# A two-layer hybrid block in split fp32: joined sums, up scale on ScalarE, copies of the transposes, and a second group of seven products in one down block

## The chip, the cores and the metric

One core of a Trainium2 chip runs the whole program. The metric is the device time of one execution in microseconds (us), the median over several runs. TensorE does the matrix products, VectorE and ScalarE prepare their operands and take up their results, SyncE and GpSimd issue the transfers from the chip's memory.

## The reference

Two residual layers over 256 rows of width 2048, float32, batch 1. Each layer is a mixer followed by a gated feed-forward network (FFN) of inner width 5632. The change lies in the FFN alone:

```python
def swiglu(hn, w_gate, w_up, w_down):
    return (jax.nn.silu(hn @ w_gate) * (hn @ w_up)) @ w_down

for layer in range(DEPTH):                       # DEPTH = 2
    h = h + (gdn_rglru_mixer if layer % 2 == 0 else fox_moba_mixer)(...)
    h = h + swiglu(rmsnorm(h, ffn_norm[layer]), ffn_w_gate[layer], ffn_w_up[layer], ffn_w_down[layer])
return rmsnorm(h, final_norm)
```

`w_gate` and `w_up` are 2048 x 5632, `w_down` is 5632 x 2048.

## The kernel before

Every float32 matrix is split into a high part (`hi`, rounded) and a low part (`lo`, the rest), and a product is three matrix products: hi with hi, hi with lo, lo with hi. A weight unit is a 128 x 1024 piece: SyncE loads it (`load`, L173), ScalarE rounds it to `whi` (L179), VectorE subtracts to get `wlo` (L180), and TensorE streams it 512 columns at a time (`Bank.add`, L409 to L411) against the transposed activations, `X` or `hid`, which are held split in the same way. One unit feeds 12 matmuls of 512 columns.

The FFN goes through 11 gate/up blocks of 512 inner columns, in three stages of 4, 4 and 3, and after each stage two down blocks (p = 0 and 1) add that stage's part to the result `h`. In this text a stage's blocks are called j0, j1, j2, j3, p0, p1. A `block` (L418) has four accumulators `F00`, `F01`, `F10`, `F11` in PSUM (128 x 512 each; the first figure is the half of the rows, the second gate or up, or the half of the down columns).

Some groups of four k-tiles are not multiplied directly (8 units, 48 matmuls) but by a Winograd form of Strassen's method (`seven`, 7 products, 42 matmuls). This needs sums of weight units on VectorE (`total`, tile `T`, L384), each split again (`halves`: `thi` on ScalarE, L376; `tlo` on VectorE, L377), one sum that a GpSimd transfer adds on the way in (L443), combinations of the activations (`combine`: tiles `cf`, `cc` and `comb`, L392 to L397), four more PSUM banks `M0` to `M3`, and at the end sums of these (`ends`, tiles `e`, L462 and L464) that are added to the `F` results. In before every gate/up block except the first uses two groups of sevens; p0 uses one, p1 two in the stages of 4 and one in the stage of 3.

After a gate/up block, SiLU of the gate goes over ScalarE (L530), the up part is added and scaled on VectorE (L533, L534), and the product is transposed back in the next block: `turn` (L508, run as a hook at the next block's third unit) has 8 transposes on TensorE into two PSUM tiles `Ph` (L503), ScalarE rounds them into `hid` (L507), and VectorE subtracts (L508). I call this place the hook. `combine` of a stage's `hid` runs from hooks as well (`late`).

A scheduler puts the instructions of each engine into one fixed order; engines wait for one another by semaphores. Buffers bound how far VectorE and ScalarE run ahead: 4 for `whi`, 3 for `wlo`, 2 each for `thi`, `tlo` and `T`, 7 for raw units.

Of the kernel before, what the change touches and what calls it, by code (L numbers as in the profile page):

```python
# [11 lines left out]
T = 256  # L12
# [35 lines left out]
def body(tc, A, out):  # L48
# [338 lines left out]
    def combine(x4):  # L387

        f = mx.tile([128, 4, T], F32, name="cf", tag="T", bufs=2)
        c = mx.tile([128, 4, 2, 128], F32, name="cc4", tag="T", bufs=2)  # L390
        r = fp.tile([128, 2, 4, 2, 128], F32R, name="comb", tag="comb", bufs=4)
        V.tensor_tensor(out=f, in0=x4[:, :, 0].bitcast(F32), in1=x4[:, :, 1].bitcast(F32), op=ALU.add)  # L392
        a11, a21, a12, a22 = (f[:, 2 * j:2 * j + 2, t * 128:(t + 1) * 128] for j in range(2) for t in range(2))
        for i, (x, y) in enumerate(((a21, a22), (a21, a11), (a22, c[:, 1]), (a12, c[:, 2]))):
            V.tensor_tensor(out=c[:, i], in0=x, in1=y, op=ALU.subtract)
        S.copy(r[:, 0], c)
        V.tensor_tensor(out=r[:, 1], in0=c, in1=r[:, 0].bitcast(F32), op=ALU.subtract)  # L397
        return r

# [14 lines left out]
    def sums():  # L414

        return [[mx.tile([128, 512], F32, name=f"e{t}{i}", tag=f"e{t}{i}", bufs=1) for i in range(2)] for t in range(2)]

    def block(src, x, comb, nd, hooks, tail=0, lead=2, trail=None):  # L418
# [74 lines left out]
    def ffn(L, then, fin=None):  # L493

        gu, dn = A[f"gu{L}"], A[f"dn{L}"]
        todo, cx, ch = [], {}, {}
# [12 lines left out]

        b = 0  # L510

        for groups in ((0, 2, 2, 2), (2, 2, 2, 2), (2, 2, 2)):
            piece = len(groups)
            hid = ogp.tile([128, 16, 2, T], F32R, name="hid", tag="hid")
            late = {4: lambda hid=hid: ch.update({0: combine(hid[:, 0:4])})}
            for j in range(piece):
                hooks = {2: turn} if todo else {}
                if b == 0:
                    hooks[5] = lambda: cx.update({0: combine(X[:, 0:4])})
                    hooks[8] = rstd  # L520
                    hooks[10] = lambda: cx.update({1: combine(X[:, 4:8])})
# [4 lines left out]
                a = e or sums()  # L526
                for t in range(2):
                    if e:
                        V.tensor_tensor(out=a[t][0], in0=F[t][0], in1=e[t][0], op=(ALU.add, ALU.subtract)[t])
                    S.activation(a[t][0], a[t][0] if e else F[t][0], AF.Silu, scale=nrm["rs"][:, t:t + 1])  # L530
                for t in range(2):
                    if e:
                        V.tensor_tensor(out=a[t][1], in0=F[t][1], in1=e[t][1], op=ALU.add)  # L533
                    V.scalar_tensor_tensor(out=a[t][0], in0=a[t][1] if e else F[t][1], scalar=nrm["rs"][:, t:t + 1],  # L534
                                           in1=a[t][0], op0=ALU.mult, op1=ALU.mult)
                    todo.append((hid, j, t, a[t][0]))
                b += 1
            u0 = 2 * (b - piece)
            for p in range(2):
                end = b == NB and p == 1  # L540
                hooks = {2: turn} if todo else {}
                if p == 0 and piece == 4:
                    hooks.update(late)

                    hooks[9] = lambda hid=hid: ch.update({1: combine(hid[:, 4:8])})
                if end and fin:
                    hooks.update({5: lambda: then(0), 6: lambda: then(1)})
                last = (3, 1, 3) if end and fin else (0, 5 if 4 in hooks else 2)
# [749 lines left out]
```

## Time and profile before

| | |
|---|---|
| median of 3 runs | 2227.28 us (2226.58 to 2227.33) |
| the profiled execution's own time | 2228.4 us |
| its span in the trace | 2226.6 us |
| TensorE busy (matmul) | 2211.8 us, 99% |
| VectorE busy | 1917.1 us, 86% |
| ScalarE busy | 1284.9 us, 58% |
| granted TensorE clock | 0.999 of full speed |

A matmul's busy time overlaps its successor's, so 99% is not by itself a full engine: the distance from one start to the next shows what a matmul costs and where TensorE waited. The two FFNs take about 445 to 1110 us and 1540 to 2218 us; the mixers lie ahead of each.

### The profile page before, as it was taken

Reading aid. Unit: us, or ns where it says so; the run is one execution under the profiler, and the core shown is the slowest. Engines: PE = TensorE matmul, PEld = TensorE weight load, DVE = VectorE, ACT = ScalarE, POOL = GpSimd, SP = SyncE. Lnnn points to the kernel's source line nnn. Section 1 sums busy time; section 2 is a strip of 40 time slices with the busy share of each in tenths; the row PEclk is TensorE's granted clock in tenths of the full one; section 3 lists DMA queues with packets and bytes.
Section 4 is the critical chain, followed back from the end, with each engine's and each line's share of the span. In section 5 each row is a group of like instructions: output and inputs, shape, how many; then the busy total and the mean of one; then the engine's idle time right before and its main releaser. Section 6 shows DMA issues by size and latency. Waiting matters only on the chain.

```text
span 2226.6 us, 30372 instructions
## 1 busy us (share of the span) xinstructions
PE 2211.8 (99%) x11002; PEld 1847.0 (83%) x11002; DVE 1917.1 (86%) x2713; ACT 1284.9 (58%) x1687; POOL 50.6 (2%) x62
## 2 busy tenths in 40 slices
PE   9999999999999999999999999999999999999998
PEld 8888888888888888888878888888888888888886
DVE  8899676679999999999966658866999999999998
ACT  6776664555555665555654444545665566555565
POOL 0000000000000000000000000000000000000000
PEclk9999999999999999999999999999999999999999
DMA  7445445677777776777665455556777777777774
GB/s 281 155 146 163 141 152 184 208 223 227 212 227 231 220 233 211 225 230 225 193 196 171 161 169 175 168 178 185 223 226 216 221 225 238 219 214 239 218 236 151
DMA packets 125992, 451.67 MB, mean 203 GB/s; under 512 B 14065, under 2 KB 15601, under 8 KB 125713
## 3 DMA queue, kind: packets, MB, share of 16 engines
q1 hardware_dynamic: 117488, 420.10, 58.3%
q0 software_dynamic: 8064, 29.36, 7.8%
q8 instruction: 86, 1.41, 0.3%
q14 instruction: 66, 0.53, 0.1%
q10 hardware_dynamic: 288, 0.27, 0.0%
HBM read 447.58 MB, written 2.10 MB: 202 GB/s over the span
## 4 chain that ended last, share of the span: by engine, by line
PE 95%; DVE 2%; issue 1%; ACT 1%; DMA 1%; DVEq 0%; ACTq 0%
PE F L411 15%; PE F L410 15%; PE F L409 15%; PE Pw L199 10%; PE Pw L204 5%; PE Px L303 5%; PE Px L304 5%; PE Px L305 5%; PE M L410 5%; PE M L411 4%; PE M L409 4%; PE Ph L503 1%; DVE wlo L180 1%; PE Psc L1068 1%; PE Pt L326 0%
## 5 line engine op out<-in xcount | busy, mean ns | idle before, releaser
L179 ACT CAST whi<-raw 128x1024 fp32r<-128x1024 f32 x720 | 755.3, 1051 | 666.8 <-PE F L411 263.8
L180 DVE TENSOR_TENSOR wlo<-raw,whi 128x1024 fp32r<-128x1024 f32 x720 | 874.5, 1219 | 189.3 <-PE Px L304 70.1
L199 PE MATMUL Pw<-X,whi 128*128 128x512 f32 x1088 | 388.3, 400 | 0.0
L409 PE MATMUL F<-whi,X 128*128 128x512 f32 x848 | 331.4, 391 | 0.0
L410 PE MATMUL F<-wlo,X 128*128 128x512 f32 x848 | 330.4, 390 | 0.0
L411 PE MATMUL F<-whi,X 128*128 128x512 f32 x848 | 330.0, 389 | 0.0
L204 PE MATMUL Pw<-X,wlo 128*128 128x256 f32 x1088 | 304.8, 280 | 1.0 <-DVE wlo L180 0.9
L376 ACT CAST thi<-T 128x1024 fp32r<-128x1024 f32 x168 | 176.6, 1051 | 124.1 <-DVE T L384 84.0
L199 PEld LDWEIGHTS Pw<-X,whi 128*128 128x128 f32 x1088 | 204.2, 188 | 47.7 <-issue 0.5
L377 DVE TENSOR_TENSOR tlo<-T,thi 128x1024 fp32r<-128x1024 f32 x168 | 205.1, 1221 | 28.0 <-ACT thi L376 27.3
L204 PEld LDWEIGHTS Pw<-X,wlo 128*128 128x128 f32 x1088 | 205.3, 189 | 2.4 <-DVE wlo L180 2.0
L409 PE MATMUL F<-whi,hid 128*128 128x512 f32 x480 | 187.5, 391 | 0.0
L411 PE MATMUL F<-whi,hid 128*128 128x512 f32 x480 | 186.9, 389 | 0.0
L410 PE MATMUL F<-wlo,hid 128*128 128x512 f32 x480 | 186.8, 389 | 0.0
L411 PEld LDWEIGHTS F<-whi,X 128*128 128x128 f32 x848 | 159.2, 188 | 33.1
L409 PEld LDWEIGHTS F<-whi,X 128*128 128x128 f32 x848 | 159.2, 188 | 32.7
L410 PEld LDWEIGHTS F<-wlo,X 128*128 128x128 f32 x848 | 159.2, 188 | 32.4
L384 DVE TENSOR_TENSOR T<-T,raw 128x1024 f32<-128x1024 f32 x112 | 136.5, 1219 | 1.1 <-DMA raw<-in_gu 0.2
L410 PE MATMUL M<-tlo,comb 128*128 128x512 f32 x336 | 131.8, 392 | 1.1 <-DVE tlo L377 1.0
L409 PE MATMUL M<-thi,comb 128*128 128x512 f32 x336 | 131.4, 391 | 0.0
L411 PE MATMUL M<-thi,comb 128*128 128x512 f32 x336 | 130.9, 390 | 0.0
L411 PEld LDWEIGHTS F<-whi,hid 128*128 128x128 f32 x480 | 90.1, 188 | 18.8
(389 smaller groups left out, 3409.5 us busy)
## 6 DMA issues: line engine op xcount, KB each, us to landing
raw<-in_gu SPq DMA_DIRECT2D x352, 512.0 KB, 4.4
raw<-in_dn SPq DMA_DIRECT2D x176, 512.0 KB, 4.4
raw<-in_w0w SPq DMA_DIRECT2D x72, 512.0 KB, 3.6
raw<-in_wo SPq DMA_DIRECT2D x64, 512.0 KB, 3.6
raw<-in_w1w SPq DMA_DIRECT2D x64, 512.0 KB, 3.6
raw<-in_gu POOLq DMA_DIRECT2D x40, 512.0 KB, 6.8
raw<-in_w1x SPq DMA_DIRECT2D x32, 512.0 KB, 3.7
raw<-in_w0x SPq DMA_DIRECT2D x16, 512.0 KB, 3.6
```

What stands on the lines that cost most here:

```text
L179: S.copy(hi, raw)
L180: V.tensor_sub(lo, raw, hi.bitcast(F32))
L199: PE.matmul(P.rearrange("p a b -> p (a b)"), hi[:, kk], X[:, k].rearrange("p a b -> p (a b)"), start=k == 0, stop=False)
L204: PE.matmul(P[:, 0], lo[:, kk], X[:, k, 0], start=False, stop=k == NK - 1)
L303: PE.matmul(Ps[t], x[:, 0, ts], hi[:, kk], start=k == 0, stop=False)
L304: PE.matmul(Ps[t], x[:, 0, ts], lo[:, kk], start=False, stop=False)
L376: S.copy(hi, t)
L377: V.tensor_sub(lo, t, hi.bitcast(F32))
L384: V.tensor_tensor(out=t, in0=a, in1=b, op=ALU.add)
L409: PE.matmul(self.t, xh, hi[:, kk], start=self.i == kk == 0, stop=False)
L410: PE.matmul(self.t, xh, lo[:, kk], start=False, stop=False)
L411: PE.matmul(self.t, xl, hi[:, kk], start=False, stop=kk == 1 and self.i == self.n - 1)
```

## The change

Four edits, all in `combine`, `sums`, `ends` and `ffn`.

1. The four `e` tiles become one tile `e` of 128 x 4 x 512. In `ends`, two of the four narrow sums are joined into one of 2 x 512 that reads `M1` twice; after down blocks the four additions of `h` become two of 1024.
2. The up part's scale moves from VectorE (L534) to a ScalarE activation, and the product of gate and up becomes one multiplication of 2 x 512.
3. The combinations of `hid` no longer add the split halves again (`cf<-hid`, L392): in `turn`, ScalarE makes two more copies of the transposes straight into a tile `cf`. The combinations move from the down block p0 and its hooks into the gate/up blocks j1 and j2 (j1 alone in the stage of 3), hook 6.
4. In the first stage of each FFN, p0 uses two groups of sevens instead of one.

```diff
+    def whole():
+        return mx.tile([128, 4, T], F32, name="cf", tag="T", bufs=2)
-    def combine(x4):
-        f = mx.tile([128, 4, T], F32, name="cf", tag="T", bufs=2)
+    def combine(f):
...
-        V.tensor_tensor(out=f, in0=x4[:, :, 0].bitcast(F32), in1=x4[:, :, 1].bitcast(F32), op=ALU.add)
...
     def sums():
-        return [[mx.tile([128, 512], F32, name=f"e{t}{i}", tag=f"e{t}{i}", bufs=1) for i in range(2)] for t in range(2)]
+        return mx.tile([128, 4, 512], F32, name="e", tag="e", bufs=1)
...
         def ends():
-            (c1, w5), (v, w7) = sums()
-            S.copy(c1, M[0].t)
-            for o, a, b, op in ((v, M[2], c1, ALU.subtract), (w5, M[1], v, ALU.add), (v, M[3], v, ALU.add), (w7, M[3], w5, ALU.add)):
-                V.tensor_tensor(out=o, in0=a.t, in1=b, op=op)
+            e = sums()
+            S.copy(e[:, 0], M[0].t)
+            V.tensor_tensor(out=e[:, 1], in0=M[2].t, in1=e[:, 0], op=ALU.add)
+            V.tensor_tensor(out=e[:, 2], in0=M[3].t, in1=e[:, 1], op=ALU.add)
+            V.tensor_tensor(out=e[:, 1::2], in0=M[1].t.rearrange("p (a n) -> p a n", a=1).to_broadcast([128, 2, 512]),
+                            in1=e[:, 1:3], op=ALU.subtract)
...
         def turn():
...
+            if j < wanted[0]:
+                cf[j] = whole()
+                for t, (P, d) in enumerate(Ps):
+                    S.copy(cf[j][:, :, t * 128:(t + 1) * 128], P)
...
-                if j == 1 and piece == 3:
-                    hooks[6] = late[4]
+                if 0 < j <= wanted[0]:
+                    hooks[6] = chs(j - 1)
...
+                for i, f in enumerate((AF.Silu, AF.Copy)):
+                    for t in range(2):
+                        if e is not None:
+                            V.tensor_tensor(out=a[:, 2 * t + i], in0=F[t][i], in1=a[:, 2 * t + i], op=ALU.add)
+                        S.activation(a[:, 2 * t + i], F[t][i] if e is None else a[:, 2 * t + i], f, scale=nrm["rs"][:, t:t + 1])
+                V.tensor_tensor(out=a[:, 0::2], in0=a[:, 1::2], in1=a[:, 0::2], op=ALU.mult)
...
-                if p == 0 and piece == 4:
-                    hooks.update(late)
-                    hooks[9] = lambda hid=hid: ch.update({1: combine(hid[:, 4:8])})
...
-                             {m: lambda m=m: ch[m] for m in range(1 + (p == 1 and piece == 4))}, piece, hooks, *last)
+                             {m: lambda m=m: ch[m] for m in range(2 if both or p == 1 and piece == 4 else 1)}, piece, hooks, *last)
...
+                    V.tensor_tensor(out=et, in0=h[:, t, c], in1=et, op=ALU.add)
```

The first place is ScalarE's order at the hook of j2 in the first FFN's first stage, with what each row waits for. Before:

```order
L179 CAST whi<-raw_5498 128x1024 [waits DMAHW4_49,DVE_49,PE_49]
L507 CAST hid<-Ph 128x4x128 [waits PE_49] x2
L376 CAST thi<-T 128x1024 [waits DVE_49]
L179 CAST whi<-raw_5525 128x1024 [waits DMAHW7_49,PE_49,Activation_49]
L376 CAST thi<-raw_5377 128x1024 [waits DMASW2_49,PE_49]
```

And of the change:

```order
L179 CAST whi<-raw_5507 128x1024 [waits DMAHW4_49,PE_49,Activation_49]
L517 CAST hid<-Ph 128x4x128 [waits PE_49] x2
L523 COPY cf<-Ph 128x4x128 [waits DVE_49] x2
L179 CAST whi<-raw_5534 128x1024 [waits DMAHW6_49,PE_49,Activation_49]
L376 CAST thi<-T 128x1024 [waits DVE_49]
L376 CAST thi<-raw_5383 128x1024 [waits DMASW2_49,PE_49,Activation_49]
```

Two copies stand between the casts of the transposes and the next `thi`, and each of the two waits for VectorE.

The second place is VectorE's order at the same hook. Before:

```order
L384 TENSOR_TENSOR T<-T,raw_5447 128x1024
L180 TENSOR_TENSOR wlo<-raw,whi 128x1024
L384 TENSOR_TENSOR T<-raw_5498,raw 128x1024
L508 TENSOR_TENSOR hid<-Ph,hid 128x4x128 x2
L377 TENSOR_TENSOR tlo<-T,thi 128x1024
L180 TENSOR_TENSOR wlo<-raw_5498,whi 128x1024
L377 TENSOR_TENSOR tlo<-raw_5377,thi 128x1024
```

And of the change:

```order
L180 TENSOR_TENSOR wlo<-raw_5456,whi 128x1024
L377 TENSOR_TENSOR tlo<-T,thi 128x1024
L180 TENSOR_TENSOR wlo<-raw,whi 128x1024
L518 TENSOR_TENSOR hid<-Ph,hid 128x4x128 x2
L384 TENSOR_TENSOR T<-T,raw_5456 128x1024
L180 TENSOR_TENSOR wlo<-raw_5507,whi 128x1024
L377 TENSOR_TENSOR tlo<-T,thi 128x1024
L377 TENSOR_TENSOR tlo<-raw_5383,thi 128x1024
```

The last sum of the first group and the first sum of the second stood ahead of the `hid` rows and now stand behind them; after the hook the two `tlo` that TensorE asks for next are the third and fourth wide rows, where they were the first and third.

## Rows read from the trace of the kernel before

**Rows 1.** The page: the span, and busy time of each engine.
```profile
span 2226.6 us, 30372 instructions
PE 2211.8 (99%) x11002; PEld 1847.0 (83%) x11002; DVE 1917.1 (86%) x2713; ACT 1284.9 (58%) x1687; POOL 50.6 (2%) x62
```

**Rows 2.** Timeline of TensorE: start, duration, line, operation, count, idle before and releaser.
```profile
578.20 0.39 PE L410 MATMUL F<-wlo,X 128*128 128x512 f32 x1
...
579.01 0.39 PE L411 MATMUL M<-thi,comb 128*128 128x512 f32 x1
...
704.30 0.39 PE L409 MATMUL F<-whi,X 128*128 128x512 f32 x1
...
717.90 0.39 PE L409 MATMUL M<-thi,comb 128*128 128x512 f32 x1
...
718.63 0.40 PE L411 MATMUL M<-thi,comb 128*128 128x512 f32 x1
...
968.62 0.39 PE L409 MATMUL F<-whi,X 128*128 128x512 f32 x1
...
970.10 0.40 PE L411 MATMUL M<-thi,comb 128*128 128x512 f32 x1
...
1810.04 0.40 PE L409 MATMUL M<-thi,comb 128*128 128x512 f32 x1
...
1811.00 0.40 PE L411 MATMUL M<-thi,comb 128*128 128x512 f32 x1
```

**Rows 3.** Waits of TensorE's weight loads, whole span: us in total, times, longest.
```profile
PEld M L410 <- DVE tlo L377: 4.0, 8, 1.2
...
PEld F L410 <- DVE tlo L377: 1.2, 6, 0.2
PEld M L409 <- DVE hid L508: 1.0, 4, 0.4
PEld M L409 <- ACT thi L376: 1.0, 4, 0.3
```

**Rows 4.** Windows of j1, j2, j3, p0, p1 of stage one: length, engines' busy, counts.
```profile
478.00:519.70 41.70, 41.70 (x190) 34.58 (x189) 37.33 (x38) 25.27 (x28) 1.73 (x2) 1.00 0.76 225
519.70:561.40 41.70, 41.70 (x190) 34.56 (x189) 39.06 (x40) 24.20 (x27) 1.73 (x2) 1.00 0.75 227
561.40:603.00 41.60, 41.52 (x187) 33.92 (x186) 40.53 (x45) 24.59 (x28) 0.86 (x1) 1.00 0.68 215
603.00:646.00 43.00, 43.00 (x196) 35.69 (x195) 40.87 (x47) 23.07 (x25) 1.72 (x2) 1.00 0.72 211
646.00:687.00 41.00, 41.00 (x183) 33.89 (x182) 38.27 (x40) 22.25 (x23) 0.86 (x1) 1.00 0.78 231
```

**Rows 5.** Timeline of VectorE behind the hook of j3, and two later rows.
```profile
572.80 1.28 DVE L508 TENSOR_TENSOR hid<-Ph,hid 128x512 fp32r<-128x512 f32 x2
574.00 1.21 DVE L377 TENSOR_TENSOR tlo<-T,thi 128x1024 fp32r<-128x1024 f32 x1
575.13 1.22 DVE L180 TENSOR_TENSOR wlo<-raw,whi 128x1024 fp32r<-128x1024 f32 x1
576.27 1.22 DVE L392 TENSOR_TENSOR cf<-hid 128x1024 f32<-128x1024 f32 x1
577.40 1.22 DVE L377 TENSOR_TENSOR tlo<-raw,thi 128x1024 fp32r<-128x1024 f32 x1
...
626.12 0.75 DVE L395 TENSOR_TENSOR cc<-cf 128x256 f32<-128x256 f32 x2
```

**Rows 6.** Waits of VectorE in the first FFN, 446 to 1100 us.
```profile
DVE tlo L377 <- ACT thi L376: 17.7, 30, 1.4
```

**Rows 7.** Timeline of all engines at the hook of j2.
```profile
528.19 1.03 PE L503 MATMUL Ph<-tab,e 128*128 128x128 f32 x8
...
529.34 1.07 ACT L507 CAST hid<-Ph 128x512 fp32r<-128x512 f32 x2
...
530.49 1.28 DVE L508 TENSOR_TENSOR hid<-Ph,hid 128x512 fp32r<-128x512 f32 x2
```

More of the change, by code (lines that the diff above doesn't have):

```diff
@@ L398, in combine, with combine_x @@
         return r
+    def combine_x(x4):
+        f = whole()
+        V.tensor_tensor(out=f, in0=x4[:, :, 0].bitcast(F32), in1=x4[:, :, 1].bitcast(F32), op=ALU.add)
+        return combine(f)
     class Bank:
@@ L495, in ffn @@
         gu, dn = A[f"gu{L}"], A[f"dn{L}"]
-        todo, cx, ch = [], {}, {}
+        todo, cx, ch, cf = [], {}, {}, {}
         def turn():
@@ L514, in ffn @@
             hid = ogp.tile([128, 16, 2, T], F32R, name="hid", tag="hid")
-            late = {4: lambda hid=hid: ch.update({0: combine(hid[:, 0:4])})}
+            both, wanted[0] = b == 0, piece - 2
+            chs = lambda m: lambda: ch.update({m: combine(cf.pop(m))})
             for j in range(piece):
@@ L518, in ffn @@
                 if b == 0:
-                    hooks[5] = lambda: cx.update({0: combine(X[:, 0:4])})
+                    hooks[5] = lambda: cx.update({0: combine_x(X[:, 0:4])})
                     hooks[8] = rstd
-                    hooks[10] = lambda: cx.update({1: combine(X[:, 4:8])})
-                if j == 1 and piece == 3:
-                    hooks[6] = late[4]
+                    hooks[10] = lambda: cx.update({1: combine_x(X[:, 4:8])})
+                if 0 < j <= wanted[0]:
+                    hooks[6] = chs(j - 1)
                 F, e = block(lambda i, u: gu[b, u, i], lambda k: X[:, k], {m: lambda m=m: cx[m] for m in range(groups[j])}, 4, hooks)
-                a = e or sums()
-                for t in range(2):
[L528 to L536, printed above, removed]
+                a = sums() if e is None else e
+                for i, f in enumerate((AF.Silu, AF.Copy)):
[4 more added lines that the diff above has]
+                V.tensor_tensor(out=a[:, 0::2], in0=a[:, 1::2], in1=a[:, 0::2], op=ALU.mult)
+                for t in range(2):
+                    todo.append((hid, j, t, a[:, 2 * t]))
                 b += 1
@@ L541, in ffn @@
                 hooks = {2: turn} if todo else {}
-                if p == 0 and piece == 4:
-                    hooks.update(late)
-                    hooks[9] = lambda hid=hid: ch.update({1: combine(hid[:, 4:8])})
                 if end and fin:
                     hooks.update({5: lambda: then(0), 6: lambda: then(1)})
-                last = (3, 1, 3) if end and fin else (0, 5 if 4 in hooks else 2)
+                last = (3, 1, 3) if end and fin else ()
                 F, e = block(lambda i, u: dn[2 * p + i, u0 + u], lambda k: hid[:, k],
-                             {m: lambda m=m: ch[m] for m in range(1 + (p == 1 and piece == 4))}, piece, hooks, *last)
+                             {m: lambda m=m: ch[m] for m in range(2 if both or p == 1 and piece == 4 else 1)}, piece, hooks, *last)
+                c = slice(2 * p * 512, (2 * p + 2) * 512)
+                for t in range(2):
+                    et = e[:, 2 * t:2 * t + 2].rearrange("p a n -> p (a n)")
+                    V.tensor_tensor(out=et, in0=h[:, t, c], in1=et, op=ALU.add)
                 hs = [[h[:, t, (2 * p + i) * 512:(2 * p + i + 1) * 512] for i in range(2)] for t in range(2)]
-                for t in range(2):
-                    for i in range(2):
-                        V.tensor_tensor(out=e[t][i], in0=hs[t][i], in1=e[t][i], op=ALU.subtract if t > i else ALU.add)
                 if end and fin:
                     with tc.manual_schedule(engines={V.engine, S.engine}):
-                        fin(lambda t, i: V.tensor_tensor(out=hs[t][i], in0=F[t][i], in1=e[t][i], op=ALU.add))
+                        fin(lambda t, i: V.tensor_tensor(out=hs[t][i], in0=F[t][i], in1=e[:, 2 * t + i], op=ALU.add))
                     continue
@@ L560, in ffn @@
                     for i in range(2):
-                        V.tensor_tensor(out=hs[t][i], in0=F[t][i], in1=e[t][i], op=ALU.add)
+                        V.tensor_tensor(out=hs[t][i], in0=F[t][i], in1=e[:, 2 * t + i], op=ALU.add)
                 if b == NB and not fin:
```

8 lines of the change are left out of this document (4 added, 4 removed).

## The prediction

> **What bounds the kernel now.** I read the page first [rows 1]: TensorE is busy for 99% of the span, VectorE for 86%, ScalarE for 58%. Since matmuls overlap, the next view is the timeline of TensorE [rows 2]: from 704.30 to 717.90 us lie 60 matmuls of 512 columns, so one start follows another after 13.60/60 = 0.2267 us. That pitch is the price of a matmul as long as its operands are there, and nearly every gap in both FFNs has it. What breaks it are five places, all in the FFNs, where TensorE waits for a `tlo` of VectorE. Over two steps, 0.453 us without a wait, it took 0.81 us at 578.20, 0.73 at 717.90, 1.48 at 968.62 and 0.96 at 1810.04; the fifth, at 1670, is the second FFN's twin of 578 and as long. The loss is 0.36 + 0.28 + 1.03 + 0.36 + 0.51 = 2.5 us. The waits of the weight loads [rows 3] give the outer bound: all that they waited for `tlo`, `thi` and `hid` is 4.0 + 1.2 + 1.0 + 1.0 = 7.2 us, in 22 waits, and a weight load runs ahead of its matmul, so not all of it was lost.
>
> So TensorE's own work is the bound, with little to win from waiting; but VectorE is close behind. The windows of five blocks [rows 4] show it busy for 37.3, 39.1, 40.5, 40.9 and 38.3 us of 41.7, 41.7, 41.6, 43.0 and 41.0, and it also idles where a `tlo` must wait for the `thi` that ScalarE makes from the sum just before: 17.7 us over 654 us [rows 6], 1.1 us in a block of 41.7 us. In j3, 40.5 + 1.1 = 41.6 is the whole window: that is where the 0.36 us at 578.20 went, and behind its hook [rows 5] stand `hid` twice, `tlo`, `wlo`, the sum `cf`, and only then the late `tlo`, at 577.40.
>
> **The change part by part.** *Matmuls.* A group of sevens has 42 matmuls where plain units have 48. One more group in each FFN removes 12 matmuls: 12 x 0.2267 = 2.72 us, wholly on the path. The other edits touch no matmul.
>
> *VectorE's work.* By starts [rows 5] a row of 1024 elements costs 1.13 us, one of 512 costs 0.60 (1.20 for two), one of 256 about 0.37 (0.75 for two). The joined sums turn 4 x 0.60 = 2.40 into 2 x 0.60 + 1.13 = 2.33, in 32 blocks; the up scale turns six narrow rows (3.6) into four and a wide one (3.53), in 20 blocks; the sums with `h` turn 8 narrow rows into 4 and 2 wide ones, 0.14 less in 12 blocks. The sums `cf` go: 10 x 1.13. A new group adds 10 wide rows where 8 plain units had 8: 2 x 2.27. In all 2.2 + 1.4 + 1.7 + 11.3 - 4.5 = 12 us less. The row of 2 x 512 that reads a bank twice is not in the trace; between 0.60 (one row of 512) and 1.28 (two rows as they stand, [rows 5]) I take the wide row's 1.13. None of this is on the path; it counts only where VectorE is late.
>
> *Where it lies.* A combination without its sum is 4 x 0.37 + 1.13 = 2.6 us, and it moves. By block [rows 4]: j1 37.3 + 2.6 - 0.1 = 39.8; j2 39.1 + 2.6 - 0.1 = 41.6; j3 40.5 - 3.7 - 0.1 = 36.7 (the first `cf` and its combination stood here); p0 40.9 - 3.7 + 2.3 - 0.2 = 39.3; p1 38.1. The sum is about the same, but j2 becomes the fullest: with 1.1 us of forced idle 42.7 us in 41.7 us. The stage of 3 and the blocks behind p1 get lighter, so the waits at 717.90, 968.62 and 1810.04 should go, and so should the two in j3: 2.5 us back.
>
> *New waits.* In j2 VectorE falls 1.0 us behind. Its order is less kind there too: two sums now stand behind `hid`, and the two `tlo` that TensorE asks for next are the third and fourth wide rows. j3 of before, filled to the brim, lost 0.36 us; j2 with 1.0 us more would lose up to 1.4, or nothing if the operands made ahead absorb it. I take 0.7, the middle, since the rows give no nearer one. There are two such stages in each FFN (the stage of 3 combines one group only, and without the sum): 4 x 0.7 = 2.8 us, with bounds 0 and 5.6.
>
> *ScalarE.* Two copies at ten hooks and two more activations in each of 22 blocks; by the two casts of 1.07 us [rows 7] a pass is 0.53, so a block gains some 1.07 + 1.07 + 1.05 = 3.2 us on 25 of 41.7 us [rows 4]. That is covered by idle time. What is not covered is the order: each copy waits for VectorE's read of the same `Ph`, and behind it stand the next `whi` and `thi`. At the hook of j2 [rows 7] the casts ended at 529.34 + 1.07 = 530.41 and VectorE read from 530.49 to 531.77. The copies would end near 532.3, so ScalarE comes free 1.9 us later. I count it at nothing beyond the 0.7 us: the `thi` behind it are asked for about 6.5 us after `Ph` began (8 transposes, 1.03 us by their row, then 24 matmuls, 5.4 us), at 528.19 + 6.5 = 534.7, and two casts after 532.3 the first is ready at 534.4. It is just in time, and each delay of VectorE's read passes on one to one.
>
> Here the Trainium skill bears on the case: *PSUM — Partial Sum Buffer*, "PSUM bank collisions raise a hardware error", says that two engines must not touch one bank and quadrant at once, reads against reads included. The trace agrees as far as it goes: the reads of `Ph` by ScalarE end at 530.41 and VectorE's begin at 530.49 [rows 7], though another row of VectorE may have set that moment. Were the copies free to read beside VectorE, they would end near 531.5, 0.8 us sooner, and the term of 2.8 us would shrink to some 0 to 2; with the rule it stands.
>
> *The sum.* The profiled execution took 2228.4 us, its span 2226.6 us. 2228.4 - 2.7 - 2.5 + 2.8 = 2226.0. The median of the runs, 2227.28 us, is 1.1 us below the profiled one, so the forecast is 2224.9 us, 2.4 us or 0.11% less. The mixers keep their order, and the tail its rows; they count nothing.
>
> **The rivals.** A difference under 0.2%, 4.5 us, is about what a measurement of this kernel can't tell from none.
>
> *All waits go.* VectorE's 12 us less is enough, j2's excess is absorbed by the buffers, and no new wait shows: 2227.3 - 2.7 - 2.5 = 2222.1 us. For it: the load of the whole stage doesn't rise and 1.0 us is less than one unit's 2.7 us. Against it: the j3 of before lost time without any excess.
>
> *Nothing comes of it.* The old waits stay, because j0 behind p1 was late for a transfer rather than for work, and j2 pays 2.8 us: 2227.3 - 2.7 + 2.8 = 2227.4 us. For it: the longest of them, 1.03 us, is one of a kind, with no twin in the second FFN. Against it: the blocks ahead of it lose work.
>
> *Slower: the copies hold up ScalarE.* At ten hooks ScalarE is free 1.9 us later, and what I called just in time is late: VectorE's `tlo` wait for `thi`, its lateness moves the next read of `Ph`, and the next copies with it. If half of the 1.9 us comes out at TensorE at every hook, that is 9.5 us: 2227.3 - 2.7 - 2.5 + 2.8 + 9.5 = 2234.4 us. It decides from about 0.7 us a hook on. For it: the waits stand in the order, and VectorE in j2 has no reserve. Against it: in j1 and in the stage of 3 the next `thi` that matters is asked for later.
>
> **How the numbers follow.** Forecast 0.48, all waits go 0.22, nothing comes of it 0.22, slower 0.08. The forecast and the third case lie within 0.2%: 0.70 for the same. All waits go gives faster by more than 4.5 us: 0.22. The last gives slower: 0.08. The forecast's own range is 2222.5 (new waits 0.4 in all) to 2227.7 (5.6 of them). The range for 8 in 10 takes in the first rival and the third, and leaves the slower one out: 2221.5 to 2229.0 us. Its ends lie beyond the cases by about half a microsecond below, and above by what a quarter of the slower rival's term would add.
>
> **What would show it.** Right: 12 fewer matmuls at a pitch of 0.2267 us; no wait left at the places in j0 behind p1; waits for `tlo` in j2 or at the hook of j3, in the first two stages of each FFN, together 2 to 4 us; VectorE's busy time 12 us lower, ScalarE's higher by some 30 us. Wrong: waits for `thi` or `tlo` behind the copies at most hooks, half a microsecond and more each; or a profile in which weight loads wait no longer at all; or VectorE's row of 2 x 512 much above 1.13 us.

## The result: 0.5% slower, and the profile after

The changed kernel takes 2238.9 us (median of 6 runs, 2234.3 to 2239.6), the kernel before beside it 2226.4 us (6 runs): ratio 1.0051, 95% interval 1.0041 to 1.0061. By that ratio it is 11.4 us longer (the medians differ by 12.5); every "us over before" below is worked out from a ratio in this way. The forecast was 2.4 us less, with a range that ended at 2229.0 us. The page of the changed kernel, against [rows 1]:

```profile
span 2237.7 us, 30300 instructions
...
PE 2218.7 (99%) x10990; PEld 1841.3 (82%) x10990; DVE 1909.6 (85%) x2637; ACT 1331.7 (60%) x1757; POOL 52.4 (2%) x64
```

TensorE has 12 matmuls fewer, as foreseen, and VectorE works 7.5 us less; yet the span grew by 11.1 us. So TensorE waits some 13.8 us more. Its timeline shows where, in the manner of [rows 2]:

```profile
595.38 0.39 PE L417 MATMUL F<-whi,X 128*128 128x512 f32 x1
595.61 0.39 PE L418 MATMUL F<-wlo,X 128*128 128x512 f32 x1
596.63 0.50 PE L417 MATMUL F<-thi,X 128*128 128x512 f32 x1 [0.64 <-ACT thi L376]
...
2193.05 0.39 PE L419 MATMUL F<-whi,hid 128*128 128x512 f32 x1
2195.51 0.49 PE L417 MATMUL F<-whi,hid 128*128 128x512 f32 x1 [2.07 <-DVE h L572]
2195.81 0.61 PE L418 MATMUL F<-wlo,hid 128*128 128x512 f32 x1
2196.22 0.63 PE L419 MATMUL F<-whi,hid 128*128 128x512 f32 x1
2196.65 0.63 PE L417 MATMUL F<-whi,hid 128*128 128x512 f32 x1
```

At 595.61, in j3, the next start comes 1.02 us later instead of 0.227; at 2193.05, where p0 ends and p1 begins in the last stage, 2.46 us later, and behind it starts stand up to 0.43 apart. The waits of the weight loads have also grown, those for ScalarE's `thi` most: 11.1 us in these rows, where [rows 3] has 1.0; those for `tlo` rose from 5.2 to 8.5:

```profile
PEld M L417 <- ACT thi L376: 7.1, 23, 0.6
PEld M L418 <- DVE tlo L377: 5.1, 12, 1.0
PEld F L417 <- ACT thi L376: 4.0, 8, 1.2
PEld F L418 <- DVE tlo L377: 3.4, 14, 0.5
```

For the comparison of many kernels I add up, for each block, the time between one start of a 512-column matmul and the next, less 0.2267 us, and call it the block's loss; a step that holds the transposes of the hook is left out. Both FFNs together, in us (1j2 is j2 of the first stage). The runs are described in the next section; u stands for the changed kernel with a part undone, b for the kernel before with a part done, a for the changed kernel altered:

| kernel | ratio to before [95%] | 1j0, 1j1 | 1j2, 1j3 | 1p0, 1p1 | 2j0, 3j0 | 2j1 | 2j2, 2j3 | 2p0, 2p1 | 3j1, 3j2 | 3p0, 3p1 | all |
|---|---|---|---|---|---|---|---|---|---|---|---|
| before | 1 | 0.8 | 1.4 | 0.2 | 2.5 | 0.5 | 0.8 | 0.2 | 1.1 | 0.8 | 8.3 |
| after | 1.0051 [41, 61] | 0.9 | 4.6 | 1.8 | 2.8 | 1.7 | 3.0 | 0.2 | 2.6 | 4.8 | 22.2 |
| b1 | 1.0027 [18, 35] | 0.7 | 3.8 | 0.2 | 2.3 | 0.6 | 2.7 | 0.2 | 1.2 | 0.8 | 12.5 |
| b2 | 1.0032 [20, 45] | 0.9 | 3.1 | 0.2 | 2.7 | 3.0 | 4.5 | 0.2 | 1.8 | 0.8 | 17.2 |
| b3 | 1.0020 [11, 30] | 5.1 | 1.1 | 0.2 | 1.8 | 0.3 | 0.8 | 0.2 | 1.3 | 0.7 | 11.5 |
| b4 | 1.0075 [62, 87] | 0.7 | 1.3 | 6.6 | 2.2 | 1.0 | 2.0 | 7.0 | 1.4 | 0.9 | 23.1 |
| b5 | 1.0013 [4, 22] | 0.7 | 1.5 | 0.3 | 1.5 | 0.6 | 3.1 | 0.3 | 1.6 | 0.8 | 10.2 |
| b6 | 1.0013 [4, 21] | 0.8 | 1.4 | 0.5 | 1.4 | 0.6 | 3.0 | 0.2 | 1.1 | 0.8 | 9.7 |
| b7 | 1.0077 [63, 90] | 0.8 | 1.5 | 8.8 | 8.6 | 0.6 | 3.0 | 0.2 | 1.0 | 0.8 | 25.4 |
| b8 | 1.0024 [15, 33] | 0.7 | 1.4 | 1.4 | 0.5 | 1.6 | 1.0 | 0.6 | 1.1 | 3.4 | 11.7 |
| b9 | 1.0071 [59, 84] | 0.7 | 2.0 | 7.0 | 1.6 | 0.8 | 2.0 | 5.1 | 1.5 | 0.8 | 21.5 |
| b10 | 1.0018 [9, 26] | 0.8 | 1.2 | 0.2 | 0.7 | 1.8 | 1.3 | 0.2 | 1.1 | 2.5 | 9.7 |
| u1 | 1.0075 [63, 88] | 0.8 | 4.9 | 1.6 | 1.8 | 1.3 | 3.0 | 8.9 | 2.1 | 0.8 | 25.2 |
| u2 | 1.0027 [15, 38] | 0.8 | 3.5 | 1.4 | 2.0 | 2.1 | 2.8 | 2.7 | 2.2 | 1.5 | 19.0 |
| u3 | 1.0040 [26, 54] | 3.4 | 1.9 | 1.9 | 1.9 | 0.6 | 4.3 | 0.7 | 1.7 | 0.9 | 17.3 |
| u4 | 1.0045 [32, 57] | 0.8 | 4.6 | 2.3 | 1.5 | 1.4 | 3.2 | 0.2 | 2.2 | 1.2 | 17.5 |
| u234 | 1.0044 [32, 57] | 0.7 | 5.4 | 0.2 | 1.3 | 0.5 | 3.3 | 0.2 | 2.3 | 5.2 | 19.0 |
| a1 | 1.0026 [17, 35] | 0.9 | 1.7 | 1.5 | 1.3 | 1.6 | 1.7 | 0.8 | 2.1 | 1.0 | 12.6 |
| a2 | 1.0028 [16, 39] | 0.8 | 1.6 | 1.7 | 2.5 | 1.3 | 1.7 | 0.2 | 2.4 | 1.1 | 13.2 |
| a3 | 1.0078 [64, 92] | 0.9 | 1.6 | 6.1 | 7.6 | 2.5 | 1.2 | 0.2 | 2.5 | 3.1 | 25.7 |

(The interval's two figures are its last digits: [41, 61] is 1.0041 to 1.0061. Losses are of one profiled run each, which for the changed kernel took 2239.5 us, near the upper end of its six; the ratio is of all runs, of b3's without one execution of 6690.6 us.) For the changed kernel the row closes: 22.2 - 8.3 - 12 x 0.2267 = 11.2 us against 11.1 us of span.

### The profile page after: what moved, and what is told of

Its sections match the earlier page's. It is cut to its first block, busy times and chain, and to the rows that moved or that the text cites. A ratio compares the mean times of both kernels' runs of the same rounds, so it can differ in the third digit from the quotient of the medians.

```text
span 2237.7 us, 30300 instructions
## 1 busy us (share of the span) xinstructions
PE 2218.7 (99%) x10990; PEld 1841.3 (82%) x10990; DVE 1909.6 (85%) x2637; ACT 1331.7 (60%) x1757; POOL 52.4 (2%) x64
## 4 chain that ended last, share of the span: by engine, by line
PE 94%; DVE 3%; issue 1%; ACT 1%; DMA 1%; DVEq 0%; ACTq 0%; SPq 0%
PE F L418 15%; PE F L417 15%; PE F L419 15%; PE Pw L199 10%; PE Pw L204 5%; PE M L418 5%; PE Px L303 5%; PE M L417 5%; PE Px L305 5%; PE Px L304 5%; PE M L419 4%; PE Ph L513 1%; DVE wlo L180 1%; PE Psc L1079 1%; PE Pt L326 0%
## 5 line engine op out<-in xcount | busy, mean ns | idle before, releaser
L376 ACT CAST thi<-T 128x1024 fp32r<-128x1024 f32 x174 | 183.4, 1054 | 143.7 <-DVE T L384 115.7
L377 DVE TENSOR_TENSOR tlo<-T,thi 128x1024 fp32r<-128x1024 f32 x174 | 212.5, 1221 | 33.3 <-ACT thi L376 32.3
L417 PE MATMUL F<-whi,hid 128*128 128x512 f32 x452 | 177.2, 392 | 2.1 <-DVE h L572 2.1
L418 PE MATMUL F<-wlo,hid 128*128 128x512 f32 x452 | 176.8, 391 | 0.0
L419 PE MATMUL F<-whi,hid 128*128 128x512 f32 x452 | 176.8, 391 | 0.0
L384 DVE TENSOR_TENSOR T<-T,raw 128x1024 f32<-128x1024 f32 x116 | 141.5, 1219 | 0.9 <-DMA raw<-in_gu 0.5
L417 PE MATMUL M<-thi,comb 128*128 128x512 f32 x348 | 138.0, 397 | 0.5 <-ACT thi L376 0.4
L418 PE MATMUL M<-tlo,comb 128*128 128x512 f32 x348 | 136.9, 393 | 0.8 <-DVE tlo L377 0.8
L419 PE MATMUL M<-thi,comb 128*128 128x512 f32 x348 | 135.7, 390 | 0.0
L417 PEld LDWEIGHTS F<-whi,hid 128*128 128x128 f32 x452 | 85.3, 189 | 20.0 <-issue 2.5
```

The source lines that it names most:

```text
L376: S.copy(hi, t)
L377: V.tensor_sub(lo, t, hi.bitcast(F32))
L384: V.tensor_tensor(out=t, in0=a, in1=b, op=ALU.add)
L417: PE.matmul(self.t, xh, hi[:, kk], start=self.i == kk == 0, stop=False)
L418: PE.matmul(self.t, xh, lo[:, kk], start=False, stop=False)
L419: PE.matmul(self.t, xl, hi[:, kk], start=False, stop=kk == 1 and self.i == self.n - 1)
```

## The experiments

**Undoing one part of the changed kernel (u1 to u4).** Each run's expectation, printed before its result, sets theories against one another. Theory A blamed ScalarE's copies, B the second group, C the joined sums at the seam of p0 and p1, D the up scale; E, added for the second round, blamed the place of the combinations.

u1, the sums with `h` narrow again:

```diff
-                    V.tensor_tensor(out=et, in0=h[:, t, c], in1=et, op=ALU.add)
+                    for i in range(2):
+                        V.tensor_tensor(out=e[:, 2 * t + i], in0=hs[t][i], in1=e[:, 2 * t + i], op=ALU.add)
```

> The changed kernel with one part undone: the sums with h stand as four rows of 512 instead of two of 1024. Theory C (order of VectorE at the seam between p0 and p1: in the stage of 3 of the second FFN TensorE waited 2.46 us at 2193 us for the sum that frees F00, and the next matmuls came at half pitch): the pause there goes and the time falls by about 3.9 us, from 2238.9 to 2235.0. Theories A, B and D (the loss is made by ScalarE's copies, by the second group, or by the up scale): the pause may stay, the time stays within 1.5 us of 2238.9.

Measured: the pause at 2193 us went (3p0, 3p1: 4.8 to 0.8), but the kernel became slower still, 16.7 us over before: p1 of the second stage now loses 4.1 us in one FFN and 4.7 in the other (2p1), at two pauses some 16 us into the block and a lower clock behind them. C is right on the place and wrong on the time. At the first of these places, where the next start after 915.75 comes 1.32 us later, ScalarE's timeline shows a late weight unit, and right behind it the `thi` that TensorE waits for:

```profile
915.02 1.05 ACT L179 CAST whi<-raw 128x1024 fp32r<-128x1024 f32 x1 [4.55 <-DMA raw<-in_dn]
915.98 1.03 ACT L376 CAST thi<-raw 128x1024 fp32r<-128x1024 f32 x1
```

The windows around it (window, length, busy time of TensorE, its weight loads, VectorE, ScalarE and GpSimd, granted clock, share of the DMA engines, GB/s):

```profile
912.00:914.00 2.00, 2.00 (x11) 1.65 (x10) 1.15 (x1) 0.00 (x0) 0.00 (x0) 1.00 1.02 268
914.00:916.00 2.00, 2.00 (x10) 1.44 (x8) 0.00 (x0) 0.98 (x2) 0.00 (x0) 1.00 1.03 416
916.00:918.00 2.00, 0.64 (x2) 0.19 (x1) 0.95 (x1) 2.00 (x4) 0.00 (x0) 1.00 0.95 387
```

From 912 to 916 VectorE is busy for 1.15 us and ScalarE for 0.98, and the DMA engines run at full share: a weight unit, not an engine, is what all wait for.

u2, the up scale on VectorE again (`scalar_tensor_tensor` for each half, as in before L534):

> The changed kernel with one part undone: the up scale and the product stand on VectorE again, one narrow row for each half. Theory D (two more activations a block stand ahead of the casts on ScalarE, so thi and whi come late and the many small waits of 0.1 to 0.4 us appear): the small waits go, some 4 to 6 us less, 2233 to 2235. Theory A (the copies of Ph hold ScalarE up) and theory B (the second group of sevens in p0 of the first stage, with its transfers): no more than 1 us either way, since ScalarE has 40% of idle time and VectorE's work stays the same; 2238 to 2240.

Measured: 6.0 us over before, 5 us less than the change: as D said. That the waits of j2 and j3 stay (3.5 and 2.8) speaks against D's mechanism.

u3, no copies; `combine` sums `hid` at the same hooks:

```diff
-            if j < wanted[0]:
-                cf[j] = whole()
...
-            chs = lambda m: lambda: ch.update({m: combine(cf.pop(m))})
+            chs = lambda m, hid=hid: lambda: ch.update({m: combine_x(hid[:, 4 * m:4 * m + 4])})
```

> The changed kernel with one part undone: no copies of Ph on ScalarE; the combinations sum hid again on VectorE, at the same hooks. Theory A (each copy waits for VectorE's read of the same Ph, and the next whi and thi stand behind it): the waits at j3 of the first stage (1.4 us in each FFN) and at j0 of the second stage shrink, 4 to 8 us less, 2231 to 2235, although VectorE has 11 us more work. Theory B (second group, transfers) or C (the seam of p0 and p1): those waits stay, and with VectorE fuller in j1 and j2 the time is the same or up to 3 us longer, 2238 to 2242.

Measured: 8.9 us over before, 2.5 less, with overlapping intervals: short of the 4 to 8 us less that A said. 1j3 got better (3.7 to 0.8), 1j1 and 2j3 worse.

u4, `both = False`:

> The changed kernel with one part undone: p0 of the first stage has one group of sevens again (12 matmuls more in all, 2.7 us of TensorE); combinations and copies stay. Theory B (the second group puts 10 wide rows and 7 late transfers where 8 plain units stood, and its loss exceeds its 2.7 us): the time falls, 2234 to 2238. Theories A, C and D: only the 12 matmuls come back, 2.7 us longer, 2241 to 2242.

Measured: 10.0 us over before, though 12 matmuls came back. So the group's 2.7 us are used up by waits in the changed kernel, as B said; its interval overlaps the change's.

No single undoing brought the time back to before's. So the parts were done one by one on the kernel before.

**One part alone (b1 to b3, and u234).** b1 moves the combinations, with their sum on VectorE; b2 also makes them from copies; b3 has the up scale alone (`S.activation(..., AF.Copy, scale=rs)` and a narrow product); u234 is the changed kernel with u2, u3 and u4 together.

```diff
-                if j == 1 and piece == 3:
-                    hooks[6] = late[4]
+                if 0 < j <= piece - 2:
+                    hooks[6] = chs(j - 1)
...
-                if p == 0 and piece == 4:
-                    hooks.update(late)
-                    hooks[9] = lambda hid=hid: ch.update({1: combine(hid[:, 4:8])})
...
-                last = (3, 1, 3) if end and fin else (0, 5 if 4 in hooks else 2)
+                last = (3, 1, 3) if end and fin else ()
```

The last edit lets p0's groups begin three units earlier. The changed kernel has it too; the section on the change doesn't list it.

> The kernel before with one part done alone: the combinations of hid stand where the changed kernel has them (at the seventh unit of j1 and j2, in the stage of 3 of j1), with their sum on VectorE; no copies, no second group, no joined sums, no up scale on ScalarE. Theory A (the copies) and theory D (the up scale): nothing of the loss is here, within 1.5 us of before; VectorE is fuller in j1 and j2 and may lose 1 to 2 us there, but p0 gains what it had lost. Theory E (the loss comes from where the combinations stand): 4 to 8 us longer than before.

> The kernel before with the combinations moved and made from ScalarE's copies of Ph, nothing else. Theory A (the copies stand behind VectorE's read of the same Ph and hold whi and thi up): 4 to 6 us longer than before, waits of about 1 us behind the hook of j3 in the first stage of each FFN; more than the kernel that only moves them. Theory D (the up scale): within 1.5 us of before, since 11 us of VectorE's work are gone.

> The kernel before with the up scale alone on ScalarE, the product on VectorE; nothing else. Theory D (two more activations at every seam between two blocks hold thi and whi up): 4 to 6 us longer than before. Theory A (the copies): within 1 us of before.

> The changed kernel with three parts undone: up scale on VectorE, no copies, one group in p0 of the first stage. What is left beside the kernel before are the joined sums and the moved combinations. Theory C (joined sums change VectorE's order at the seams): 3 to 5 us longer than before and than the kernel that only moves the combinations. Theories A and D: within 1.5 us of the latter.

Measured: b1 6.0 us, b2 7.1, b3 4.5, u234 9.8 us over before. A falls as the main cause: the copies add 1.1 us to the moved combinations, less than the intervals' width. E holds: the place of the combinations alone costs more than half of the whole, in 1j2, 1j3 (+2.4) and 2j2, 2j3 (+1.9). D's price holds, but at one place only, where j1 of the first stage follows j0 (0.8 to 5.1). TensorE's timeline of b3 there:

```profile
492.70 0.39 PE L411 MATMUL F<-thi,X 128*128 128x512 f32 x1
493.64 0.49 PE L409 MATMUL M<-thi,comb 128*128 128x512 f32 x1 [0.55 <-ACT thi L376]
494.89 0.50 PE L410 MATMUL M<-tlo,comb 128*128 128x512 f32 x1 [0.76 <-DVE tlo L377]
```

The changed kernel has nothing at that place (0.9), so b3's price isn't a term of its time.

**Which move, and which sum (b4 to b7).** b4: the joined sums alone. b5: only the first combination moved, to j1. b6: the two in j1 and j3 (`if j == 1 or j == 3: hooks[6] = chs(j // 2)`). b7: b6 with the second group in p0.

> The kernel before with the joined sums alone (the row that reads a bank twice, and two rows of 1024 instead of four of 512 for the sums with h); combinations, up scale and groups as before. Theory C (F00 is freed later, since its sum with h now waits for the whole chain of sums: a pause of TensorE of 2 to 3 us at the seam of p0 and p1 in the stage of 3 of the second FFN, and half clock behind it): 3 to 5 us longer than before, with the pause at that place alone. Theory E (all of the loss stands where the combinations stand): within 1 us of before.

> The kernel before with only the first combination of hid moved, to the seventh unit of j1; the second stays in p0 and p0 keeps its late groups. Moving both cost 6 us, most of it in j2 and j3. Theory E1 (the second combination, in j2, fills VectorE there, and the loss comes out at j3): less than 2 us longer than before, and j3 as before or better. Theory E2 (the loss comes from p0's groups of sevens, which begin three units earlier): also less than 2 us. Theory E3 (any combination ahead of the hook costs the next block 1 us): 3 us longer.

> The kernel before with the first combination at the seventh unit of j1 and the second at that of j3 instead of j2, p0's groups three units earlier. Theory E1 (j2 is too full with a combination in it): VectorE's work by block is then 41, 39, 41, 37 us, j2 and j3 keep the excess of before, and the time is within 2 us of before. Theory E2 (p0's groups that begin earlier) or E3 (any block behind a combination): 4 to 6 us longer, as when both were moved to j1 and j2.

> As the kernel with the combinations in j1 and j3, and a second group of sevens in p0 of the first stage (12 matmuls less, 2.7 us). If its ten wide rows on VectorE are covered in p0 and p1: 2.7 us less than that kernel, 1 to 3 us less than before. If the second group pays as it does in the changed kernel (0.4 us in p0 and 0.4 us in p1 of each FFN): 1.2 us less than the kernel without it, about the time of before.

Measured: b5 and b6 2.9 us over before, b4 16.7, b7 17.1. E1 holds for the second half of b1's 6 us: with the second combination out of j2, 1j2 and 1j3 keep the loss of before (1.4), though the 2.9 us left are more than E1's 2. They stay with the first combination, in 2j2 and 2j3 (E3 in part). E2 falls, since b6, with p0's groups three units earlier, costs no more than b5, which left them in their place. Joined sums and second group both cost 14 us and more here, nearly all of it in p0, p1 or just behind: no theory foresaw that size. In b4, where TensorE pauses at 661.84, ScalarE waits for a weight unit as in u1 (its timeline), and the DMA engines are again at a share of 0.91 to 1.03 (658 to 664 us), though VectorE is busy here until 662 us:

```profile
661.99 1.05 ACT L179 CAST whi<-raw 128x1024 fp32r<-128x1024 f32 x1 [2.50 <-DMA raw<-in_dn]
662.94 1.04 ACT L376 CAST thi<-raw 128x1024 fp32r<-128x1024 f32 x1
```

**The joined sums taken apart, and the second combination moved within the changed kernel (b8 to b10, a1).** b8 has the one tile `e` and the signs, all rows narrow; b9 adds the row that reads `M1` twice, b10 the rows of 1024 with `h`. a1 is the changed kernel with the second combination in j3, made from a sum on VectorE instead of copies.

```diff
-            both, wanted[0] = b == 0, piece - 2
-            chs = lambda m: lambda: ch.update({m: combine(cf.pop(m))})
+            both, wanted[0] = b == 0, 1
+            chs = lambda m, hid=hid: lambda: ch.update({m: combine_x(hid[:, 4 * m:4 * m + 4]) if m else combine(cf.pop(m))})
...
-                if 0 < j <= wanted[0]:
-                    hooks[6] = chs(j - 1)
+                if j == 1 or j == 3:
+                    hooks[6] = chs(j // 2)
```

> The kernel before with the four sums kept in one tile of 4x512 instead of four tiles, and the signs that go with it; every row of VectorE has its old size. Theory C1 (the size of the joined rows makes the pauses: they stand in one piece in front of the rows that free raw buffers): within 1.5 us of before. Theory C2 (it is the one tile: the next block's sums may not begin before the last reader of all four halves is done, and that shifts VectorE's order): most of the 16.7 us of the joined sums, 2238 to 2244, with the pauses of 2 to 4 us in p1.

> The kernel before with the joined row that reads a bank twice (and the one tile), sums with h narrow as before. Theory C1a (the row of 2 x 512 is the cause): 10 us or more longer than before, pauses in p1. Theory C1b (the two rows of 1024 with h are): within 2 us of the kernel with the one tile alone.

> The kernel before with the two rows of 1024 with h (and the one tile), the sums of a block's end narrow as before. Theory C1b (F00, and the rows behind it, wait for a row that needs the whole chain of sums): 10 us or more longer than before, pauses in p1 behind late transfers. Theory C1a: within 2 us of the kernel with the one tile alone.

> The changed kernel with the second combination of hid at the seventh unit of j3 instead of j2, from a sum on VectorE (the first stays in j1, from ScalarE's copies). Theory E1 (a combination in j2 fills VectorE there, and j2 and j3 of the first two stages lose 5.3 us more than before): these waits fall to 2 us or less in all, and the time by 3 us or more, unless p0, which follows j3 and has two groups now, takes it back as in the kernel with the combinations in j1 and j3 and two groups. Theory A (the copies): also less, since half of them go, but j1 stays as it is and j2 and j3 fall by no more than half.

Measured: b8 5.3, b9 15.8, b10 4.0 us over before. The one tile alone costs more than C1 said and less than C2. On the kernel before it is the row that reads the bank twice that costs most (C1a), and yet not by its own price: it is busy for 1.22 us, as any wide row, in b9 and in the changed kernel alike (b9's groups by line: count, busy time, mean ns of one, idle time before):

```profile
L465 DVE TENSOR_TENSOR e<-M,e 128x1024 f32<-128x1024 f32 x32 | 39.2, 1224 | 0.8
```

a1 is 5.8 us over before, 5.6 less than the change: 1j2 and 1j3 fall from 4.6 to 1.7, 2j2 and 2j3 from 3.0 to 1.7, as E1 said, though it had 2 us in all and 3.4 are left. a1 also has fewer copies, so by itself it doesn't part the place from them; the place alone is what b6 has against b1, both without copies, and there it is worth 3.1 us.

**Do the repairs add up (a2, a3)?** a2 is a1 with the up scale on VectorE, a3 is a2 with narrow sums at a block's end.

> The changed kernel with two parts altered: the second combination at the seventh unit of j3, from a sum on VectorE, and the up scale on VectorE again. If the two repairs add up (5.6 us for the place of the combination, 5.3 us for the up scale): 11.4 - 10.9 = 0.5 us longer than before. If they repair the same waits: 4 to 6 us longer than before, as the first of them alone.

> As the kernel with the combination in j3 and the up scale on VectorE, and the sums at a block's end narrow again (two rows of 512 instead of the row that reads a bank twice). Theory C1a inside the changed kernel (that row costs there too, as it did alone on the kernel before): 3 us or more less than without this edit, so below the time of before. If the row matters only where the combinations stand in p0 as before: within 1.5 us of the kernel without this edit. All that is then left of the change are the second group (2.7 us less of TensorE), the first combination from copies, and the rows of 1024 with h.

Measured: a2 6.2 us over before, a3 17.4. They don't add up: u2's 5 us are worth nothing on top of a1. Both theories on a3 miss: the row that cost b9 some 10 us more than b8 now saves 11. a3, without it, is with b7 the slowest of all, by waits in p0 and p1 of the first stage and in j0 behind them (13.7 us in these columns). No kernel that was run beats the one before.

**What the second combination does.** GpSimd's timeline has the transfer that adds a weight unit on its way in (start, duration, idle before and releaser). Before:

```profile
554.78 0.86 POOL L443 DMA_DIRECT2D raw<-in_gu  x1 [22.82 <-DMA raw<-in_gu]
573.41 0.86 POOL L443 DMA_DIRECT2D raw<-in_gu  x1 [17.77 <-ACT thi L376]
```

The changed kernel:

```profile
565.70 0.86 POOL L451 DMA_DIRECT2D raw<-in_gu  x1 [26.93 <-DVE T L384]
578.25 0.86 POOL L451 DMA_DIRECT2D raw<-in_gu  x1 [11.69 <-ACT thi L376]
```

And a1:

```profile
555.93 0.86 POOL L451 DMA_DIRECT2D raw<-in_gu  x1 [25.26 <-DMA raw<-in_gu]
578.14 0.86 POOL L451 DMA_DIRECT2D raw<-in_gu  x1 [21.35 <-DVE T L384]
```

j3's first such transfer overwrites a unit that VectorE's first `T` of the group reads, and in all three kernels it begins 0.5 us behind the end of that `T`. With the combination in j2 the `T` stands behind all of the block's end. VectorE in the changed kernel:

```profile
551.35 0.75 DVE L397 TENSOR_TENSOR cc<-cf 128x256 f32<-128x256 f32 x2
...
555.63 1.23 DVE L399 TENSOR_TENSOR comb<-cc,comb 128x1024 fp32r<-128x1024 f32 x1
...
562.81 1.22 DVE L548 TENSOR_TENSOR e<-e 128x1024 f32<-128x1024 f32 x1
563.95 1.22 DVE L384 TENSOR_TENSOR T<-raw,raw 128x1024 f32<-128x1024 f32 x1
```

and in a1:

```profile
554.18 1.22 DVE L384 TENSOR_TENSOR T<-raw,raw 128x1024 f32<-128x1024 f32 x1
```

So the first group's transfer comes 11 us later and the two stand 12.6 us apart instead of 18.6. ScalarE then waits for weights in the changed kernel's j3, the second time just ahead of the pause at 595.61, and the `thi` of that pause stands right behind (in a1 no wait for a weight there is over 1.7 us):

```profile
575.84 1.05 ACT L179 CAST whi<-raw 128x1024 fp32r<-128x1024 f32 x1 [3.15 <-DMA raw<-in_gu]
...
594.58 1.05 ACT L179 CAST whi<-raw 128x1024 fp32r<-128x1024 f32 x1 [4.38 <-DMA raw<-in_dn]
595.54 1.04 ACT L376 CAST thi<-T 128x1024 fp32r<-128x1024 f32 x1
```

In the eight kernels with a combination in j2 this transfer is issued at 565.1 to 567.0 us, in the twelve without at 553.5 to 556.2, and 1j3 of the first FFN loses 0.4 to 2.1 against 0.2 to 0.8 us. u3, with 0.4 in spite of a late transfer, shows that the lateness goes with the loss but is not enough for it. Nor is the way from the late transfer to the pause shown: the second group's transfer, the one ahead of the pause, is issued at the same time as in a1. What differs is that a1 has the `thi` of that product at 589.12, ahead of the down weight. Why the row went there was not tried; in the program `cf`, `cc` and `T` share two buffers, so `T` can't begin while a combination holds both.

## Why the prediction was wrong

- **The 12 matmuls** are right: 2.7 us, at the same pitch.
- **"The two `tlo` that TensorE asks for next are the third and fourth wide rows ... I take 0.7"**: neither the size nor the place came out. j2 and j3 of the first two stages lost 5.4 us more than before, (4.6 + 3.0) - (1.4 + 0.8), where the forecast had 2.8 less the 0.7 that j3 was to regain; its bound of 5.6, less the 0.7, didn't hold it. j2, where VectorE was to fall behind, lost only 1.0 of this. The 4.4 us of j3 are not at its hook: the pause at 595.61 comes 25 us behind the transposes.
- **The sum of VectorE's rows by block** (*Where it lies*, with "so should the two in j3: 2.5 us back") is the step that failed. It made j2 the fullest block, put the new waits there and counted nothing elsewhere: 2.8 us of new waits less 2.5 of old ones, 0.3 in all, where TensorE waited 13.8 us more. By that sum j3 did get lighter: in windows of nearly the lengths of [rows 4], j2, j3 and p0 show 40.5, 39.0 and 42.3 us of VectorE (third of the busy times), where the forecast had 41.6, 36.7 and 39.3.

```profile
519.70:561.40 41.70, 41.70 (x188) 34.03 (x187) 40.46 (x43) 28.00 (x32) 0.86 (x1) 1.00 0.71 224
561.40:604.30 42.90, 42.26 (x187) 33.63 (x186) 39.04 (x38) 25.89 (x29) 2.59 (x3) 1.00 0.77 225
604.30:647.30 43.00, 43.00 (x193) 35.07 (x193) 42.26 (x43) 26.60 (x29) 1.73 (x2) 1.00 0.79 228
```

  Yet j3's loss went from 1.2 to 3.7 us in the first stage and from 0.3 to 2.1 in the second, over the two FFNs. Its two old waits for `tlo` did go; the new pause comes from a `thi` that stands in ScalarE's order behind a cast whose weight was late. The forecast never followed L443, the loads and ScalarE's order past the moved step. Of the waits behind p1, the one at 968.62 went, as foreseen; 2j0 lost 1.2 us more (2j0 and 3j0 together 0.3).
- **"A new group adds 10 wide rows where 8 plain units had 8"** is a wrong count. A group of four k-tiles is four plain units (48 matmuls, 12 to a unit), not eight; the section on the kernel before has the same slip. So it adds six wide rows, not two. The groups by line have 718 `wlo` after 720, and `tlo` and `T` rise by 8 and 6. Of `wlo` and the `tlo` from `T`, before and after:

```profile
L180 DVE TENSOR_TENSOR wlo<-raw,whi 128x1024 fp32r<-128x1024 f32 x720 | 874.5, 1219 | 189.3 <-PE Px L304 70.1 <-PE Pw L204 45.7 <-issue 28.4
L377 DVE TENSOR_TENSOR tlo<-T,thi 128x1024 fp32r<-128x1024 f32 x168 | 205.1, 1221 | 28.0 <-ACT thi L376 27.3
...
L180 DVE TENSOR_TENSOR wlo<-raw,whi 128x1024 fp32r<-128x1024 f32 x718 | 872.5, 1220 | 196.9 <-PE Px L304 68.3 <-PE Pw L204 44.3 <-issue 32.8
L377 DVE TENSOR_TENSOR tlo<-T,thi 128x1024 fp32r<-128x1024 f32 x174 | 212.5, 1221 | 33.3 <-ACT thi L376 32.3
```

  Twelve rows at 1.13 us are 13.6 us, not 4.5: by the forecast's own sum VectorE's work falls by 3 us and not by 12 (its busy time fell by 7.5), and p0 comes to 40.9 - 3.7 + 6.8 - 0.2 = 43.8 us of 43.0, not to 39.3. The block that was to get lighter was the fullest. What that costs is not shown by itself: u4, without the second group, loses as much in 1p0 and 1p1, while on b6 the group costs 14 us (b7).
- **Nothing for the joined sums.** Their price was right, their place was not weighed. F00 at 2193 us is freed by rows that stand almost in one piece (VectorE's timeline):

```profile
2190.14 1.22 DVE L473 TENSOR_TENSOR e<-M,e 128x1024 f32<-128x1024 f32 x1
2191.28 1.21 DVE L180 TENSOR_TENSOR wlo<-raw,whi 128x1024 fp32r<-128x1024 f32 x1
2192.41 2.35 DVE L564 TENSOR_TENSOR e<-h,e 128x1024 f32<-128x1024 f32 x2
2194.68 2.47 DVE L572 TENSOR_TENSOR h<-F,e 128x512 f32<-128x512 f32 x4
```

  That is 4.0 us of the 13.8 (3p0, 3p1). More than 1.2 us stand in that column only for kernels with the one tile of sums (six of thirteen, b8 with its narrow rows among them), so the wide rows aren't needed for it; why the other seven are spared stayed open.
- **The range**: a quarter of the slower rival's 9.5 us above the case "nothing comes of it", 2227.4, is 2229.8 and not 2229.0; the result lies beyond both.
- **The rest**: 1p0 and 1p1 1.6, 2j1 1.2, 3j1 and 3j2 1.5 us, all counted at nothing. The first isn't simply the second group's: with one group u234 has 0.2 there, but u4 has 2.3.
- **The rival "the copies hold up ScalarE"** gave 2234.4 us, the nearest of all to the result, but mostly by luck. The wait is there, behind VectorE's read of the same `Ph` (ScalarE's timeline):

```profile
489.11 1.19 ACT L523 COPY cf<-Ph 128x512 f32<-128x512 f32 x2 [0.70 <-DVE hid L518]
```

  but b2 against b1 puts it at 1.1 us for all ten hooks. What the prediction took from the Trainium skill, *PSUM — Partial Sum Buffer*, "PSUM bank collisions raise a hardware error" (two engines must not touch one bank and quadrant at once) agrees with this row, which `hid` releases; but the program orders the two reads by a semaphore, so no run here shows what the chip would do without it.

Open is why single parts cost 14 to 17 us alone (b4, b9, and b7 over b6) and the whole 11. Five kernels lie near 17 us (b4, b7, b9, u1, a3), and in each of them TensorE stands in p1 or right behind it. Their traces share one picture there, that of u1: at each place where TensorE lost more than 0.9 us in p1 of the first two stages or in 2j0, the `thi` that it waited for stands in ScalarE's order right behind a `whi` whose weight had not landed, and ScalarE had waited 2.1 to 5.4 us for it; the second pause comes behind the `tlo` from that same `thi`. In a3, where TensorE pauses at 710.36:

```profile
709.78 1.05 ACT L179 CAST whi<-raw 128x1024 fp32r<-128x1024 f32 x1 [4.93 <-DMA raw<-in_gu]
710.73 1.03 ACT L376 CAST thi<-T 128x1024 fp32r<-128x1024 f32 x1
```

That the scheduler's order of a few rows around these transfers decides it fits this, and fits b9 and a3, where one edit has opposite signs; but no run held the order still and changed the rows alone, so it is argued and not shown.

## What to carry to other kernels

Where an engine is 97% full (40.46 of 41.70 us) and also frees the buffers of the loads, the sum of its work per block doesn't tell the time: follow, for each moved step, when the row that sets off the next transfer comes, and what is then late. A part's effect measured alone is no term of the whole there: of 6.0, 1.1, 4.5 and 16.7 us the change paid 11. Look at the order that the edit really gave at the two or three transfers that run closest, before counting saved rows: in an engine's fixed order one cast whose input is late holds up every cast behind it. And count added rows in the trace or the program, unit by unit; here a group of four units was taken for eight.

## What the hardware showed that was not expected

After a pause TensorE's clock can fall: behind the 2.46 us at 2193.05, eight matmuls stand 0.41 to 0.43 us from the next instead of 0.227, and the granted clock of the stretch is 0.57 (near the lower level of 1.2 GHz against 2.4). The pause of 1.02 us at 595.61 had no such end: behind its first matmul starts stand 0.23 to 0.27 apart. In u1, two pauses of 1.32 and 1.26 us with one matmul between them (915.75 to 918.33) did: the granted clock from 918 to 920 us is 0.59. TensorE's windows at the longer one:

```profile
2193.00:2195.50 2.50, 0.43 (x2) 0.03 (x2) 2.50 (x4) 0.11 (x1) 0.00 (x0) 1.00 0.70 208
2195.50:2199.50 4.00, 3.99 (x11) 3.14 (x12) 3.92 (x5) 2.91 (x7) 0.00 (x0) 0.57 0.05 15
```

An activation of 512 elements takes longer than the 0.53 us that two casts of `Ph` had suggested: it is busy for 0.72 us in the changed kernel. The kernel before had shown it: its 40 SiLU activations of this shape took 721 ns on the mean (L530). With activations at that price, and with six more casts for the two new groups (eight `thi` more, two `whi` fewer), which the forecast left out, ScalarE's busy time rose by 47 us, not by 30. The groups by line:

```profile
L547 ACT ACTIVATE e<-e,rs 128x512 f32<-128x512 f32 x80 | 56.1, 722 | 25.5 <-DVE e L546 24.3
```
